# State space on Trainium2: imaginary coefficients and gate weights' low parts on GpSimd, rotation and scan in place in a PSUM bank, last norm's mean taken off early

## The chip, the cores and the metric

One Trainium2 chip, one core of it. The metric is the device time of one launch in microseconds. A core has five engines, each with an instruction list of its own that it works through in order: TensorE (PE, matmuls), VectorE (DVE), ScalarE (ACT), GpSimd (POOL) and SyncE (SP), which here issues every DMA. They wait for one another by semaphores. Matmuls write into eight PSUM banks of 128 x 512 fp32 (`bank0` to `bank7` in the rows); in this kernel GpSimd works on tiles in SBUF alone.

## What is computed

A sequence of 512 tokens with 1024 channels goes through two blocks of two layers each. The change touches the first layer's mixer, a state-space model, and the last layer norm.

```python
u = h @ w_in
a = exp(lam * step)
b, c = f(lam, step) * b, c
x[l] = a * x[l - 1] + b @ u[l]
y = real(c @ x) + d_skip * u
z = gelu(y)
val, gate = split(z @ w_glu)
x = x + val * sigmoid(gate)
...
h = layernorm(DEEPNORM_ALPHA * h + y, ln_g[layer], ln_b[layer])
```

Here `a`, `b`, `c` and the state are complex, with 64 groups of 16 channels and 64 states in each. The layer norm subtracts the mean over the 1024 channels, divides by the standard deviation, scales by `ln_g` and adds `ln_b`.

## The kernel before, in words

Activations lie with channels on partitions: eight tiles `x0` to `x7` of 128 x 512. A large matmul is done as three fp32r passes, hi x hi, lo x hi and hi x lo: the hi part of a weight (`wh`) is a ScalarE copy to fp32r, the lo part (`wl`) a VectorE subtraction (`wconv`, line 615), from the raw weights (`wr`, two buffers) that a DMA brings (`wload`).

**State space.** The projection by `w_in` has eight blocks of 128 channels. Blocks 0 to 2 are multiplied in plain fp32 from raw weights, with no wait for the first norm; blocks 3 to 7 take the three passes. Block m's result is scaled by the norm into `u` (VectorE), written to DRAM and read back in another layout. The scan over 512 tokens is cut into 64 chunks of 8. For each of the eight groups of channels m the kernel builds:
- P[m] and Q[m] (`s5_p`, `s5_q` through `s5_cprod`, line 965), powers of `a` times `b` and `c`. Each is four products of 128 x 512, two for the real part and two for the imaginary part, and two additions or subtractions. The products go into a ring of four buffers (tag `s5t`; in the order below `s5_45`, `s5_46`, `s5_53`, `s5_54`), and read the powers from bank 7, where ScalarE has copied them. `Bt` and `Ct` (`s5_58`, `s5_59` for even m, `s5_61`, `s5_62` for odd m) hold `b` and `c`.
- K[m], eight small matmuls of `Bh` (`s5_60`, `s5_63`) with Q[m], and P[m] transposed by eight PE transposes through a bank that ScalarE empties.
- `s5_x` (line 1049): the chunk inputs, 16 small matmuls into bank 6; a rotation by tables of cosine and sine that turns the complex recurrence into a real one; one scan over the chunks; a rotation back, giving the state `st`. Each rotation is two VectorE products and two GpSimd halves.
- `s5_y`: K[m] and `st` with Q[m] times `u`, in PE; then `s5_o`, the transposes back and the gelu. `glu_part` multiplies with `w_glu` as the groups become ready, its weights split in `load_glu` (line 1208).

The tables (`s5_table`, line 929), four in all, are built on GpSimd by doubling, one for two groups: at each step two products and two halves, up to 512 wide. The first norm's inverse root is GpSimd's power (`rsqrt`, line 737; tile `sm4_r1`, `sm_r` in the profile); PE spreads it over the partitions by four transposes, and VectorE needs it for `u`.

**What sets the order.** All instructions of the program are first collected by the class `Plan`, which estimates each one's duration and due time, and then lists them engine by engine: what stands in an engine's list is not the order in which the code is written. Everything is issued from one line, L263, so the profile's rows tell groups apart by tile and shape, not by line. A moved or retyped instruction can therefore move others in all five lists.

**The last norm.** `ln_half` (line 1721) runs for the two halves of the tokens. PE sums x and its squares over channels by matmuls with `ones`; VectorE forms mean and variance; GpSimd takes the power; VectorE multiplies by the mean; four transposes spread the inverse root and the product mean x inverse root. Then for each chunk x is multiplied by the first and the second is subtracted (on GpSimd for the first chunk, else on VectorE), ScalarE applies gain and bias, and a DMA stores it.

Of the kernel before, what the change touches and what calls it, by code (L numbers as in the profile page):

```python
# [20 lines left out]
P = 128  # L21
# [505 lines left out]
class Net:  # L527
# [86 lines left out]

    def wconv(self, raw, ncol, gain=None, cuts=1):
        nc = self.nc
# [8 lines left out]
        for c in range(0, ncol, w):  # L625
            p = slice(c, c + w)
            nc.scalar.activation(hi[:, p], raw[:, p], AF.Copy)
            nc.vector.tensor_tensor(lo[:, p], raw[:, p], hi[:, p], ALU.subtract)
        return hi, lo
# [334 lines left out]

    def s5_cprod(self, pool, out, x, tb, op0, op1, swap, E):


        V = self.nc.vector

        def prod(r, q):  # L970
            t = pool.tile([P, 4, 8, 16], F32, name=self.n("t"), tag="s5t", bufs=4)
            V.tensor_tensor(t, tb[:, :, q].unsqueeze(3).to_broadcast([P, 4, 8, 16]),
                            x[:, :, r].unsqueeze(2).to_broadcast([P, 4, 8, 16]), ALU.mult)
            return t.rearrange("p w j k -> p w (j k)")
# [4 lines left out]
        yield  # L979
        a, b = prod(1, 0), prod(0, 1)  # L980
        yield
# [4 lines left out]
    def s5_q(self, pool, m, ld):  # L986

        q = pool.tile([P, 4, 2, P], F32, name=self.n("Q"), tag="s5Q", bufs=3)
        return q, self.s5_cprod(pool, q, ld[1], self.powers[:, 1, m % 4 * 4 : m % 4 * 4 + 4], ALU.add, ALU.subtract, True,
                                (self.nc.vector, self.nc.gpsimd))  # L990

# [57 lines left out]
    def s5_x(self, pool, m, us, pt):  # L1049
# [68 lines left out]
    def layer0_mix(self, pool):  # L1118
# [602 lines left out]
    def ln_half(self, pool, h, g, b, hs=None, out=None):  # L1721

        nc, V, G = self.nc, self.nc.vector, self.nc.gpsimd
        p = self.psum("o")
        pairs = [(0, self.acc["s"]), (1, self.acc["n"])]
# [22 lines left out]
        for m in range(KC):  # L1748
# [524 lines left out]
```

## Time and profile before

| | us |
|---|---|
| median of 3 runs | 1833.55 (1832.9 to 1834.58) |
| the profiled execution's own time | 1832.58 |
| its span in the trace | 1830.8 |
| PE busy | 1788.1 (98%) |
| VectorE busy | 1153.1 (63%) |
| ScalarE busy | 840.9 (46%) |
| GpSimd busy | 431.3 (24%) |
| mean granted PE clock, of 2.4 GHz | 0.994 |

The span is what the trace shows; the profiled execution's own time holds 1.8 us more around it and lies 1.0 us below the median. Busy shares are means over the whole program: GpSimd's 24% is nearly 100% from 30 to 120 us and little after 160. The state-space stage takes about the first 156 us; from there PE is hardly ever idle until the last 10 us.

### The profile page before, as it was taken

How to read it: one execution, taken by the hardware profiler on the slowest of the kernel's cores; microseconds unless marked ns; L12 is line 12 of the kernel's file. 1: busy time of each engine (PE TensorE's matmuls, PEld its weight loads, DVE VectorE, ACT ScalarE, POOL GpSimd, SP SyncE). 2: the span in 40 equal slices, each digit the busy share in tenths (PEclk: the TensorE clock that was granted, in tenths of full speed). 3: DMA queues.
4: the chain of work that ended last, by engine and by line, in shares of the span. 5: the costliest groups of instructions: out<-in, count | busy, mean ns of one | idle time of the engine just before them, and what ended most of it. 6: DMA issues, size and time to landing. Idle time of an engine off the chain costs nothing.

```text
span 1830.8 us, 26476 instructions
## 1 busy us (share of the span) xinstructions
PE 1788.1 (98%) x10020; PEld 1448.8 (79%) x10020; DVE 1153.1 (63%) x2344; ACT 840.9 (46%) x1603; POOL 431.3 (24%) x518
## 2 busy tenths in 40 slices
PE   7999999999999999999999999999999999999997
PEld 4767888888888776678888888897878898878877
DVE  9994364344355688755444434583897875498886
ACT  4333332122223477734322223364677745476764
POOL 7981111001012176611100101230022030012104
PEclk8999999999999999999999999999999999999999
DMA  4542332332323220022233333332122122211113
GB/s 133 148 105 88 93 101 92 94 99 87 101 91 93 84 81 17 23 75 92 93 92 93 94 102 92 101 117 93 58 70 71 58 92 93 88 52 58 59 64 110
DMA packets 73135, 157.84 MB, mean 86 GB/s; under 512 B 26416, under 2 KB 34864, under 8 KB 73008
## 3 DMA queue, kind: packets, MB, share of 16 engines
q1 hardware_dynamic: 73008, 156.15, 27.7%
q8 instruction: 79, 1.29, 0.3%
q14 instruction: 48, 0.39, 0.1%
HBM read 150.81 MB, written 4.72 MB: 85 GB/s over the span
## 4 chain that ended last, share of the span: by engine, by line
PE 79%; DVE 9%; ACT 4%; POOL 2%; issue 1%; DMA 1%; SPq 0%; ACTq 0%; DVEq 0%; POOLq 0%
PE bank L263 79%; DVE bl L263 3%; DVE wl_r L263 1%; ACT bl L263 1%; DVE s L263 1%; ACT bh L263 1%; DVE x L263 1%; ACT wh_r L263 1%; DVE ml L263 1%; ACT ml L263 1%; DMA wr_r<-w_out 0%; POOL yq_r L263 0%; DVE bank L263 0%; POOL s L263 0%; POOL sm_r L263 0%
## 5 line engine op out<-in xcount | busy, mean ns | idle before, releaser
L263 ACT ACTIVATE wh_r<-wr_r 128x1024 fp32r<-128x1024 f32 (+2 forms) x269 | 277.4, 1031 | 586.8 <-PE bank L263 538.5
L263 PE MATMUL bank<-xl_r,wh_r 128*128 128x512 f32 (+1 forms) x1304 | 498.7, 386 | 0.0
L263 PE MATMUL bank<-xh_r,wl_r 128*128 128x512 f32 (+1 forms) x1304 | 497.7, 385 | 0.5 <-DVE wl_r L263 0.4
L263 PE MATMUL bank<-xh_r,wh_r 128*128 128x512 f32 (+1 forms) x1304 | 496.3, 386 | 0.8 <-ACT wh_r L263 0.7
L263 DVE TENSOR_TENSOR wl_r<-wr_r,wh_r 128x1024 fp32r<-128x1024 f32 (+2 forms) x269 | 367.0, 1365 | 152.5 <-ACT wh_r L263 144.9
L263 PEld LDWEIGHTS bank<-xh_r,wl_r 128*128 128x128 f32 x1304 | 245.4, 189 | 53.6 <-issue 3.8
L263 PEld LDWEIGHTS bank<-xh_r,wh_r 128*128 128x128 f32 x1304 | 245.1, 189 | 53.3 <-ACT wh_r L263 1.8
L263 PEld LDWEIGHTS bank<-xl_r,wh_r 128*128 128x128 f32 x1304 | 245.5, 189 | 50.4 <-issue 2.3
L263 PE MATMUL bank<-ff,wh_r 128*128 128x512 f32 (+1 forms) x816 | 226.1, 365 | 0.3 <-ACT ff L263 0.3
L263 DVE TENSOR_TENSOR ff<-bank,ff 128x512 f32<-128x512 f32 x88 | 60.9, 692 | 224.3 <-PE bank L263 224.2
L263 POOL TENSOR_TENSOR ff<-ff,ff 128x512 f32<-128x512 f32 x44 | 62.6, 1424 | 591.2 <-DVE ff L263 576.0
L263 PE MATMUL bank<-bh,wh_r 128*128 128x512 f32 (+1 forms) x656 | 171.8, 349 | 1.4 <-ACT wh_r L263 1.2
L263 PEld LDWEIGHTS bank<-ff,wh_r 128*128 128x128 f32 x816 | 145.6, 188 | 28.0 <-DVE ff L263 1.0
L263 POOL TENSOR_TENSOR acc_r<-acc_r,sq_r 128x256 f32<-128x256 f32 (+1 forms) x63 | 78.5, 1247 | 305.4 <-ACT sq_r L263 251.8
L263 PE MATMUL bank<-ff,wl_r 128*128 128x512 f32 (+1 forms) x408 | 146.8, 364 | 0.4 <-DVE wl_r L263 0.4
L263 DVE TENSOR_TENSOR x<-x,bank 128x256 f32<-128x256 f32 (+1 forms) x112 | 57.5, 531 | 128.3 <-PE bank L263 128.3
L263 PEld LDWEIGHTS bank<-bh,wh_r 128*128 128x128 f32 x656 | 111.5, 188 | 16.7 <-ACT wh_r L263 1.7
L263 POOL TENSOR_TENSOR s<-s,s 128x512 f32<-128x512 f32 (+6 forms) x136 | 108.4, 827 | 19.1 <-DVE s L263 16.7
L263 PE MATMUL bank<-bh,wl_r 128*128 128x512 f32 (+1 forms) x328 | 112.0, 351 | 0.0
L263 ACT ACTIVATE ff<-ff 128x512 f32<-128x512 f32 x88 | 55.1, 627 | 74.4 <-POOL ff L263 68.9
L263 PEld LDWEIGHTS bank<-ff,wl_r 128*128 128x128 f32 x408 | 76.2, 188 | 13.9 <-DVE wl_r L263 0.6
L263 POOL TENSOR_TENSOR bl<-bl,bh 128x512 f32<-128x512 f32 x16 | 20.7, 1292 | 254.2 <-DVE bl L263 244.4
(272 smaller groups left out, 2753.8 us busy)
## 6 DMA issues: line engine op xcount, KB each, us to landing
wr_r<-w_gu SPq DMA_DIRECT2D x88, 512.0 KB, 3.5
wr_r<-w_in2f SPq DMA_DIRECT2D x48, 512.0 KB, 3.3
wr_r<-w_dn SPq DMA_DIRECT2D x37, 448.0 KB, 3.3
wr_r<-w_out SPq DMA_DIRECT2D x22, 512.0 KB, 3.3
wr_r<-w_dn SPq DMA_DIRECT2D x16, 512.0 KB, 3.5
wr_r<-w_in2v SPq DMA_DIRECT2D x16, 512.0 KB, 3.7
wr_r<-w_glu SPq DMA_DIRECT2D x12, 512.0 KB, 3.5
wr_r<-w_o SPq DMA_DIRECT2D x8, 512.0 KB, 3.3
```

Source lines behind the costliest of these rows:

```text
L263: lambda: f(*[real(v) for v in a], **{x: real(v) for x, v in k.items()}), load, rows, idle))
```

## The change

1. `load_glu`: the eight `wl` of the `w_glu` parts (128 x 512) go from VectorE to GpSimd.
2. `s5_q`: both products of Q's imaginary part go to GpSimd, which reads the powers from SBUF (`af`, `s5_52` in the order) instead of bank 7; the addition of Q's real part goes to GpSimd, too. P stays as it was.
3. `s5_x`: ScalarE builds a tile `sg` with minus sine and sine (two copies of 128 x 256 per group). Each rotation is now three VectorE operations of 128 x 512, two of them in place in bank 6; the scan runs in place there; the four GpSimd halves per group go.
4. The second half of the last norm has a function of its own, `ln_last`. Two more matmuls spread the sum of x over all partitions; VectorE subtracts the mean while the power is under way; two transposes instead of four, one multiplication per chunk, and gain and bias on VectorE for three of the eight chunks.

```diff
-    def wconv(self, raw, ncol, gain=None, cuts=1):
+    def wconv(self, raw, ncol, gain=None, cuts=1, eng=None):
...
-            nc.vector.tensor_tensor(lo[:, p], raw[:, p], hi[:, p], ALU.subtract)
+            (eng or nc.vector).tensor_tensor(lo[:, p], raw[:, p], hi[:, p], ALU.subtract)
...
-    def s5_cprod(self, pool, out, x, tb, op0, op1, swap, E):
+    def s5_cprod(self, pool, out, x, tb, op0, op1, swap, E, sb=None):
...
-        def prod(r, q):
+        def prod(r, q, V=V, tb=tb):
...
-        a, b = prod(1, 0), prod(0, 1)
+        by = (V, tb) if sb is None else (self.nc.gpsimd, sb)
+        a, b = prod(1, 0, *by), prod(0, 1, *by)
...
-                                (self.nc.vector, self.nc.gpsimd))
+                                (self.nc.gpsimd, self.nc.gpsimd), self.af[:, 4 * m : 4 * m + 4])
...
+        sg = pool.tile([P, 4, 2, NCH], F32, name=self.n("sg"), tag="s5sg", bufs=2)
+        nc.scalar.activation(sg[:, :, 0], tab[:, :, 1], AF.Copy, scale=-1.0)
+        nc.scalar.activation(sg[:, :, 1], tab[:, :, 1], AF.Copy)
         yield
-        a, b, y, z = tmp("ra"), tmp("rb"), tmp("ry"), x4
+        a = tmp("ra")
         V.tensor_tensor(a, x4, cs, ALU.mult)
-        V.tensor_tensor(b, x4, sn, ALU.mult)
-        G.tensor_tensor(y[:, :, 0], a[:, :, 0], b[:, :, 1], ALU.add)
-        G.tensor_tensor(y[:, :, 1], a[:, :, 1], b[:, :, 0], ALU.subtract)
+        V.tensor_tensor(x4, x4, sg, ALU.mult)
+        V.tensor_tensor(x4, x4, a[:, :, ::-1], ALU.add)
         yield
         f = lambda v: v.rearrange("p j r c -> p (j r c)")
-        V.tensor_tensor_scan(xp, f(dz), f(y), 0.0, ALU.mult, ALU.add)
+        V.tensor_tensor_scan(xp, f(dz), xp, 0.0, ALU.mult, ALU.add)
         yield
-        a2, b2 = tmp("ra"), tmp("rb")
-        V.tensor_tensor(a2, z, cs, ALU.mult)
-        V.tensor_tensor(b2, z, sn, ALU.mult)
+        a2 = tmp("ra")
+        V.tensor_tensor(a2, x4, cs, ALU.mult)
+        V.tensor_tensor(x4, x4, sg, ALU.mult)
         l = slice(0, NCH - 1)
-        G.tensor_tensor(st[:, :, 0, 1:], a2[:, :, 0, l], b2[:, :, 1, l], ALU.subtract)
-        G.tensor_tensor(st[:, :, 1, 1:], a2[:, :, 1, l], b2[:, :, 0, l], ALU.add)
+        V.tensor_tensor(st[:, :, :, 1:], x4[:, :, :, l], a2[:, :, ::-1, l], ALU.add)
...
-            wa[k] = self.wconv(raw, S)
+            wa[k] = self.wconv(raw, S, eng=G)
...
+        if h and out is not None:
+            yield from self.ln_last(g, b, out)
+            return
...
+    def ln_last(self, g, b, out):
...
+        for a, src in enumerate((self.acc["s"], self.acc["x"])):
+            nc.tensor.matmul(sx[:, :256], self.ones.to_broadcast([P, P]), src[:, t], start=a == 0, stop=a == 1)
...
+        self.rsqrt(r, v)
+        rb = self.psum("s")
+        for i in range(2):
+            nc.tensor.transpose(rb[:, i * P : (i + 1) * P], r[:, i : i + 1].to_broadcast([P, P]), self.ident)
+        nc.urgent = False
+        for m in range(KC):
+            x = self.x[m][:, t]
+            V.scalar_tensor_tensor(x, sx[:, :256], -1.0 / D, x, ALU.mult, ALU.add)
+        for m in range(KC):
+            yield
+            x = self.x[m][:, t]
+            V.tensor_tensor(x, x, rb[:, :256], ALU.mult)
+            if m in (2, 5, 7):
+                V.tensor_scalar(x, x, self.col(g, m), self.col(b, m), ALU.mult, ALU.add)
+            else:
+                nc.scalar.activation(x, x, AF.Identity, bias=self.col(b, m), scale=self.col(g, m))
+            nc.sync.dma_start(out[m][:, t], x)
```

The plan turns this into other lists on every engine. Three places of them matter below. In the rows, `wr_r0_5` and `wr_r1_29` are the two buffers for raw weights, and what stands in brackets is what an instruction waits for: queues of DMAs, or the engines (`Activation` is ScalarE).

**SyncE, after the loads of the first inputs.** In the list before, the raw weights of blocks 2, 3, 4 and 5 of `w_in` stand one behind the other, and only then comes the next `Bt`:

```order
L263 DMA wr_r0_5_87<-w_in 128x1024 [waits DMAHW1_49,PE_49]
L263 DMA wr_r1_29_95<-w_in 128x1024 [waits DMAHW2_49,PE_49]
L263 DMA wr_r0_5_87<-w_in 128x1024 [waits DMAHW3_49,DMAHW1_49,PE_49]
L263 DMA wr_r1_29_95<-w_in 128x1024 [waits DMAHW4_49,DMAHW2_49,DVE_49]
L263 DMA s5_58_298<-Bt 128x128 [waits DMAHW5_49,DVE_49]
```

In the changed list these are the loads of block 2, then `Bt` and `Ct` for group 2, then blocks 3 and 5, `Bt` for group 3, and blocks 7 and 4:

```order
L263 DMA wr_r0_5_87<-w_in 128x1024 [waits DMAHW1_49,PE_49]
L263 DMA s5_58_298<-Bt 128x128 [waits DMAHW2_49,DVE_49]
L263 DMA s5_59_299<-Ct 128x128 [waits DMAHW3_49,DVE_49,Pool_49]
L263 DMA wr_r1_29_95<-w_in 128x1024 [waits DMAHW4_49,PE_49]
L263 DMA wr_r1_29_95<-w_in 128x1024 [waits DMAHW5_49,DMAHW4_49,DVE_49]
L263 DMA s5_61_301<-Bt 128x128 [waits DMAHW6_49,DVE_49]
L263 DMA wr_r1_29_95<-w_in 128x1024 [waits DMAHW7_49,DMAHW5_49,DVE_49]
L263 DMA wr_r0_5_87<-w_in 128x1024 [waits DMAHW1_49,DMAHW0_49,PE_49]
```

Block 3's load (waiting only for PE, which has read block 1 from that buffer) now stands behind a load that waits for VectorE and GpSimd, and block 4's behind that of block 7, which waits for VectorE.

**GpSimd, around the first norm's power** (`sm4_r1`). Before, the power stands between the two last 512-wide products of the first table (`s5_56`, `s5_57`; the table is `s5_24`), and the two additions for P[0] (into `s5_64`) follow it:

```order
L263 TENSOR_TENSOR s5_56_296<-s5_24_264,s5_42_282 128x512 [waits DVE_49,Pool_49]
L263 TENSOR_TENSOR sm4_r1_76_115<-sm4_r0_74_114,mhalf_81 128x4 [waits DVE_49]
L263 TENSOR_TENSOR s5_57_297<-s5_24_264,s5_42_282 128x512
L263 TENSOR_TENSOR s5_64_304<-s5_45_285,s5_46_286 128x4x128 [waits DVE_49]
L263 TENSOR_TENSOR s5_24_264<-s5_56_296,s5_57_297 128x8x32 [waits Pool_49]
L263 TENSOR_TENSOR s5_56_296<-s5_25_265,s5_42_282 128x32 [waits Pool_49]
L263 TENSOR_TENSOR s5_24_264<-s5_56_296,s5_57_297 128x8x32
L263 TENSOR_TENSOR s5_57_297<-s5_25_265,s5_42_282 128x32 [waits Pool_49]
L263 TENSOR_TENSOR s5_64_304<-s5_53_293,s5_54_294 128x4x128 [waits DVE_49]
L263 TENSOR_TENSOR s5_25_265<-s5_56_296,s5_57_297 128x8x2 [waits Pool_49]
```

After the change, the two rows of 512 and the real addition of P[0] are already past when this piece begins; the power follows the whole first table and the first products of the second (`s5_25`), and behind it come the two imaginary products of Q[0] (`s5_53` and `s5_54` from `s5_52` and `Ct`, `s5_59`):

```order
L263 TENSOR_TENSOR s5_24_264<-s5_56_296,s5_57_297 128x8x32 [waits Pool_49]
L263 TENSOR_TENSOR s5_56_296<-s5_25_265,s5_42_282 128x32 [waits Pool_49]
L263 TENSOR_TENSOR s5_24_264<-s5_56_296,s5_57_297 128x8x32
L263 TENSOR_TENSOR s5_57_297<-s5_25_265,s5_42_282 128x32 [waits Pool_49]
L263 TENSOR_TENSOR sm4_r1_76_115<-sm4_r0_74_114,mhalf_81 128x4 [waits DVE_49]
L263 TENSOR_TENSOR s5_25_265<-s5_56_296,s5_57_297 128x8x2 [waits Pool_49]
L263 TENSOR_TENSOR s5_64_304<-s5_53_293,s5_54_294 128x4x128
L263 TENSOR_TENSOR s5_25_265<-s5_56_296,s5_57_297 128x8x2
L263 TENSOR_TENSOR s5_53_293<-s5_52_292,s5_59_299 128x512 [waits DMAHW0_49,Pool_49]
L263 TENSOR_TENSOR s5_56_296<-s5_25_265,s5_42_282 128x64 [waits Pool_49]
L263 TENSOR_TENSOR s5_57_297<-s5_25_265,s5_42_282 128x64
L263 TENSOR_TENSOR s5_54_294<-s5_52_292,s5_59_299 128x512
```

The power has moved back by six operations, the products of Q[0] are new, and the real and the imaginary addition of Q[0] (`s5_28`) follow 13 and 18 operations behind the last row, the real and imaginary additions of P[1] 34 and 36 behind it.

**VectorE, behind the first norm.** Before, the four products of Q[0] with its real addition, the `wl` of blocks 4 and 5 and the first products of P[1]:

```order
L263 TENSOR_TENSOR s5_45_285<-bank7_76,s5_59_299 128x512 [waits DMAHW1_49,Activation_49,Pool_49]
L263 TENSOR_TENSOR s5_46_286<-bank7_76,s5_59_299 128x512
L263 TENSOR_TENSOR s5_32_272<-bank0_69,s5_35_275 128x512 [waits DVE_49]
L263 TENSOR_TENSOR wl_r1_137_123<-wr_r0_5_87,wh_r1_135_122 128x1024 [waits DMAHW4_49,DMAHW5_49,DMAHW3_49,Activation_49]
L263 TENSOR_TENSOR s5_53_293<-bank7_76,s5_59_299 128x512 [waits Pool_49]
L263 TENSOR_TENSOR s5_28_268<-s5_45_285,s5_46_286 128x4x128 [waits DVE_49]
L263 TENSOR_TENSOR s5_54_294<-bank7_76,s5_59_299 128x512
L263 TENSOR_TENSOR wl_r2_144_126<-wr_r1_29_95,wh_r2_142_125 128x1024 [waits DMAHW4_49,Activation_49]
L263 TENSOR_TENSOR s5_45_285<-bank7_76,s5_61_301 128x512 [waits Activation_49]
L263 TENSOR_TENSOR s5_46_286<-bank7_76,s5_61_301 128x512
```

Now, from the `wl` of block 3 (`wl_r0`) on:

```order
L263 TENSOR_TENSOR wl_r0_130_120<-wr_r1_29_95,wh_r0_128_119 128x1024 [waits DMAHW4_49,Activation_49]
L263 TENSOR_TENSOR s5_45_285<-bank7_76,s5_61_301 128x512 [waits DMAHW2_49,Pool_49]
L263 TENSOR_TENSOR s5_46_286<-bank7_76,s5_61_301 128x512 [waits DVE_49]
L263 TENSOR_TENSOR s5_53_293<-bank7_76,s5_61_301 128x512 [waits Pool_49]
L263 TENSOR_TENSOR s5_54_294<-bank7_76,s5_61_301 128x512
L263 TENSOR_TENSOR wl_r2_144_126<-wr_r1_29_95,wh_r2_142_125 128x1024 [waits DMAHW5_49,Activation_49]
L263 COPY s5_35_275<-bank6_75 128x512 [waits PE_49]
L263 TENSOR_TENSOR s5_32_272<-bank0_69,s5_35_275 128x512 [waits DVE_49]
L263 TENSOR_TENSOR s5_33_273<-bank1_70,s5_35_275 128x512
L263 TENSOR_TENSOR s5_45_285<-bank7_76,s5_62_302 128x512 [waits Activation_49,Pool_49]
L263 TENSOR_TENSOR s5_46_286<-bank7_76,s5_62_302 128x512
L263 TENSOR_TENSOR wl_r1_137_123<-wr_r0_5_87,wh_r1_135_122 128x1024 [waits DMAHW1_49,DMAHW3_49,DMAHW0_49,Activation_49]
```

The `wl` of block 5 (`wl_r2`) has come ahead of the one of block 4 (`wl_r1`), and stands behind products of P[1] into `s5_53` and `s5_54`, which wait for GpSimd to have read these two buffers for Q[0]; the `wl` of block 4 stands behind the real products of Q[1], which wait for GpSimd's real addition of P[1].

## Rows read from the trace of the kernel before

**Rows 1.** The page, part 1: busy us, share of span, instructions per engine.
```profile
PE 1788.1 (98%) x10020; PEld 1448.8 (79%) x10020; DVE 1153.1 (63%) x2344; ACT 840.9 (46%) x1603; POOL 431.3 (24%) x518
```
**Rows 2.** Windows: stretch, us, busy PE, PEld, DVE, ACT, POOL (x), PEclk, DMA share, GB/s.
```profile
30.00:38.60 8.60, 0.50 (x2) 0.19 (x1) 8.53 (x23) 0.67 (x1) 8.21 (x11) 0.74 0.17 62
38.60:45.00 6.40, 6.32 (x19) 5.05 (x20) 5.85 (x10) 3.48 (x6) 6.24 (x8) 0.55 0.29 94
60.00:100.00 40.00, 36.57 (x422) 26.92 (x422) 38.98 (x59) 12.29 (x26) 38.67 (x51) 1.00 0.46 117
100.00:156.00 56.00, 52.12 (x709) 40.65 (x705) 45.65 (x63) 18.54 (x33) 38.06 (x44) 0.97 0.36 95
156.00:1820.00 1664.00, 1650.30 (x8703) 1351.26 (x8699) 1007.17 (x2028) 780.24 (x1491) 306.37 (x349) 1.00 0.27 83
```
**Rows 3.** Waits of PE from 20 to 160: us in total, times, longest.
```profile
PE bank L263 <- POOL sm_r L263: 7.5, 1, 7.5
PE bank L263 <- DVE s L263: 3.9, 4, 1.4
PE bank L263 <- ACT s L263: 2.5, 1, 2.5
```
**Rows 4.** Timeline at the start: start us, us, engine; in brackets, idle before and releaser.
```profile
29.62 1.04 ACT L263 ACTIVATE wh_r<-wr_r 128x1024 fp32r<-128x1024 f32 x1
...
37.16 1.47 POOL L263 TENSOR_TENSOR sm_r<-sm_r,mhalf 128x4 f32<-128x4 f32 x1
...
38.68 1.11 PE L263 MATMUL bank<-ident,sm_r 128*128 128x128 f32 x4 [7.47 <-POOL sm_r L263]
```
**Rows 5.** Timeline: loads of `w_in` by SyncE (SPq), and the first `wl`.
```profile
21.39 0.33 SPq L263 DMA_DIRECT2D wr_r<-w_in  x1
...
38.61 1.21 DVE L263 TENSOR_TENSOR wl_r<-wr_r,wh_r 128x1024 fp32r<-128x1024 f32 x1
39.85 0.33 SPq L263 DMA_DIRECT2D wr_r<-w_in  x1
```
**Rows 6.** DMA issues up to 70 us: KB each, median us from issue to landing.
```profile
wr_r<-w_in SPq DMA_DIRECT2D x7, 512.0 KB, 3.6
```
**Rows 7.** Timeline of GpSimd: one row per shape, and three longer ones.
```profile
38.60 2.12 POOL L263 TENSOR_TENSOR s<-s,s 128x512 f32<-128x512 f32 x1
...
40.69 1.57 POOL L263 TENSOR_TENSOR s<-s,s 128x512 f32<-128x512 f32 x1
...
42.21 0.74 POOL L263 TENSOR_TENSOR s<-s,s 128x256 f32<-128x256 f32 x1
...
45.51 1.23 POOL L263 TENSOR_TENSOR s<-s,s 128x16 f32<-128x16 f32 x1
...
47.00 0.30 POOL L263 TENSOR_TENSOR s<-s,s 128x64 f32<-128x64 f32 x1
...
48.09 0.25 POOL L263 TENSOR_TENSOR s<-s,s 128x32 f32<-128x32 f32 x1
...
49.86 0.41 POOL L263 TENSOR_TENSOR s<-s,s 128x128 f32<-128x128 f32 x1
...
50.22 1.31 POOL L263 TENSOR_TENSOR s<-s,s 128x512 f32<-128x512 f32 x1
```
**Rows 8.** Groups by form, 40 to 156, GpSimd and VectorE: busy us, mean ns.
```profile
L263 POOL TENSOR_TENSOR s<-s,s 128x512 f32<-128x512 f32 x31 | 44.3, 1434 | 1.5 <-DVE s L263 0.8 <-PE bank L263 0.4
...
L263 DVE TENSOR_TENSOR s<-bank,s 128x512 f32<-128x512 f32 x102 | 64.4, 678 | 3.4 <-ACT bank L263 1.5 <-POOL s L263 1.4 <-PE bank L263 0.2
```
**Rows 9.** Timeline of PE: block 4's third matmul, and the stage's last small matmuls.
```profile
48.06 0.39 PE L263 MATMUL bank<-xh_r,wl_r 128*128 128x512 f32 x1
...
152.99 3.15 PE L263 MATMUL bank<-s,s 128*64 128x128 f32 x48
```
**Rows 10.** Timeline of the tail: the last power, and the last scalings on ScalarE.
```profile
1820.69 0.72 POOL L263 TENSOR_TENSOR sm_r<-sm_r,mhalf 128x2 f32<-128x2 f32 x1 [2.22 <-DVE sm_r L263]
...
1823.37 4.42 ACT L263 ACTIVATE x<-x,cols 128x256 f32<-128x256 f32 x8 [0.84 <-POOL x L263]
```

More of the change, by code (lines that the diff above doesn't have):

```diff
@@ L1059, in s5_x @@
         tab = self.tab[m // 2][:, 4 * (m % 2) : 4 * (m % 2) + 4]
-        cs, sn = (tab[:, :, a : a + 1].to_broadcast([P, 4, 2, NCH]) for a in range(2))
+        cs = tab[:, :, 0:1].to_broadcast([P, 4, 2, NCH])
         tmp = lambda nm: pool.tile([P, 4, 2, NCH], F32, name=self.n(nm), tag="s5" + nm, bufs=1)
@@ L1739, in ln_half @@
         V.tensor_tensor(c[:, 2:4], mu, c[:, 0:2], ALU.mult)
-        if h and out is not None:
-            nc.behind(self.stored)
         yield
@@ L1762, in ln_half @@
             V.tensor_tensor(lo, x, hi, ALU.subtract)
+    def ln_last(self, g, b, out):
+        nc, V = self.nc, self.nc.vector
+        t = HALF[1]
+        sx = self.psum("s")
+        p = self.psum("o")
+        for a, src in enumerate((self.acc["s"], self.acc["x"])):
+            nc.tensor.matmul(sx[:, :256], self.ones.to_broadcast([P, P]), src[:, t], start=a == 0, stop=a == 1)
+        pairs = [(0, self.acc["s"]), (1, self.acc["n"]), (0, self.acc["x"]), (1, self.acc["q"])]
+        for a, (j, src) in enumerate(pairs):
+            for i in range(2):
+                nc.tensor.matmul(p[:, 2 * j + i : 2 * j + i + 1], src[:, (2 + i) * P : (3 + i) * P],
+                                 self.ones, start=a == i == 0, stop=a == 3 and i == 1)
+        yield
+        nc.urgent = True
+        mu, m2, v, r = (self.small(2) for _ in range(4))
+        V.tensor_scalar(mu, p[:, 0:2], 1.0 / D, None, ALU.mult)
+        V.tensor_scalar(v, p[:, 2:4], 1.0 / D, LN_EPS, ALU.mult, ALU.add)
+        V.tensor_tensor(m2, mu, mu, ALU.mult)
+        V.tensor_tensor(v, v, m2, ALU.subtract)
+        nc.behind(self.stored)
+        self.rsqrt(r, v)
+        rb = self.psum("s")
+        for i in range(2):
+            nc.tensor.transpose(rb[:, i * P : (i + 1) * P], r[:, i : i + 1].to_broadcast([P, P]), self.ident)
[4 more added lines that the diff above has]
+        for m in range(KC):
+            yield
+            x = self.x[m][:, t]
[5 more added lines that the diff above has]
+            nc.sync.dma_start(out[m][:, t], x)
     def halves(self, add, order, pool, g, b, hs=None, out=None, nxt=None):
```

## The prediction

> **What bounds the kernel now.** The page first: TensorE (PE) is busy 98% of the span [rows 1], so a change counts only where PE waits, runs at its lower clock, or is handed work later. Next the waits by stage: after 156 us PE idles 13.7 of 1664 us [rows 2], so what the state-space stage gains or loses before 156 reaches the end one for one. In that stage PE idles 8.1 us from 30 to 38.6, runs to 45 at a mean granted clock of 0.55 (a mixture of 1.2 and 2.4 GHz, right behind the idle stretch), and then idles 3.4 us from 60 to 100 and 3.9 us from 100 to 156, with the clock at 0.97 in the last stretch [rows 2]. Its longest wait, 7.5 us, is for GpSimd's power that ends the first norm (`sm_r`); the later ones are mostly for VectorE (3.9) and once for ScalarE (2.5) [rows 3]. GpSimd is the other full engine: 38.7 of 40 us from 60 to 100, 38.1 of 56 after that [rows 2]. Last come single rows of the start, because the order of four queues changes there.
>
> **The start: a queue is blocked.** Before, the raw weights of block 3 of `w_in`, the first that is split, are asked for at 21.39 [rows 5]; their high part is on ScalarE at 29.62 and PE only lacks the norm, whose power runs 37.16 to 38.6 [rows 4]. That SyncE issues strictly in turn is seen at 39.85: the next load starts as `wl` ends (38.61 + 1.21) [rows 5]. After the change the load of block 3 stands behind that of `Ct`, which waits until GpSimd has read the old `Ct` in both imaginary products of Q[0]. Those are new on GpSimd. So I walk GpSimd's list.
>
> The power starts later by what is now ahead of it: the second 512-wide table product (2.12), the real add of P[0] (1.57), two halves of 256 (0.74 each) and two products of 32 (0.25 each) [rows 7], 5.7 us. One sum of squares goes ahead of the tables into idle time; I credit one 512-wide row, 1.3. Start 37.16 + 5.7 - 1.3 = 41.5. It took 1.47 here and 0.72 in the tail [rows 4, 10]; with 1.1 it ends at 42.6. From there to the second product of Q[0] the list has three operations of 512 (1.31 each), two of 64 (0.30) and two of 16 (at most the 0.25 of a 32) [rows 7]: 5.0, so 47.6. Two issues of 0.33 follow one another; the load lands 3.6 after its own issue [rows 5, 6], at 51.6; `wh` takes 1.04 [rows 4]. Block 3 starts at **52.7**; before, all but its first matmul followed the stall that ended at 38.68 [rows 4].
>
> The second hold is block 4. Its load now stands behind the load of block 7, which waits for VectorE's `wl` of block 5, and that stands behind P[1]'s imaginary products, which wait for buffers until GpSimd's imaginary add of Q[0]. From 47.6 to that add GpSimd has four operations of 512, four of 256, four of 128, two of 64 and four of 32, at 1.31, 0.74, 0.41, 0.30 and 0.25 [rows 7]: 11.4, so 59.0. To the real add of P[1] come two of 512, two of 256, four of 128, four of 64 and four of 32 or less: 7.9, so 66.9. On VectorE: 59.0, two products of 0.68 [rows 8], `wl` of 1.21 [rows 5], 61.6; load issued and landed 65.5; `wh` 66.6. The `wl` of block 4 stands behind Q[1]'s real products, which wait for the real add of P[1]: 66.9 + 2 x 0.68 + 1.21 = **69.5**.
>
> At 69.5 PE starts block 4's third matmul. Before it did so at 48.06 [rows 9]. PE is then ahead by K[0] and half of P[1]'s transposes: eight small matmuls at 3.15/48 us each [rows 9] and four transposes of at most 1.11 [rows 4], some 1.0 us together with what is halved. Delay: 69.5 - 49.1 = 20.4. What PE lost later before can be recovered: 7.3 of idle time and 0.03 of 52 us of clock, 1.6 [rows 2]. That leaves 11.5. New waits are next: K[1] needs seven more 512-wide GpSimd operations (66.9 + 9.2 = 76.1), about 1 us beyond PE's own work. VectorE gets to the first rotation only after P[2]'s imaginary products, which wait for that same add; counting from there its twelve rows at 0.68, one `wl` at 1.21 and the scan at twice 0.68, the first state is ready near 87, while 45 matmuls of 512 columns (0.21 each at 2.4 GHz), some 67 small ones at 3.15/48 and the 1 us bring PE there about 84.5: 1.5 to 2.5, of which I take the lower, as consecutive rows overlap. Sum for the stage: **+14**. The last small matmuls of the stage, at 152.99 before [rows 9], would run near 167.
>
> **The steady part.** Per group of channels GpSimd loses four rotation halves (at most 4 x 0.74) and gains two products, one add and one `wl`, four rows of 512 (5.2): +2.3, or some 18 us over eight groups. From 60 to 156 it has 19.3 us idle [rows 2], so it fits, with nothing left over; VectorE is the cover for PE here, no longer GpSimd. VectorE loses two products, an add and a `wl` and gains two adds: -1.4 by its 0.68. No row has a VectorE operation that reads and writes a bank; below, one costs like the read alone (0.68), above I double it, since both ends are banks. I take 0.68, the nearest row; doubled, four per group add 2.7 us to VectorE, which rival 3 takes up. The new ScalarE copies (two of 256 columns) are hidden beside the two thirds of the stage in which ScalarE idles [rows 2], except the four at the start, which stand ahead of the first `wh`; the blocked load covers them.
>
> **How fast is GpSimd beside VectorE?** The clean 512-wide row is 1.31, the mean in the stage 1.43 [rows 7, 8]; a 16-wide one took 1.23 [rows 7] where VectorE subtracted two SBUF tiles. I use clean rows, since the change leaves VectorE few operations with two SBUF inputs; by the mean 21 of them to K[1] cost 2.5 more, which goes into the upper end. The Trainium skill (SBUF — State Buffer, section Who interferes with whom) says that a VectorE instruction with two SBUF inputs and a GpSimd one that reads SBUF exclude each other, and that one with at most one SBUF input does not contend. The 1.23 agrees; by that rule the sum stands at clean rows, +14, and by the mean at +16.5.
>
> **The tail.** The mean is subtracted while the power (0.72) runs, so behind it come one multiply per chunk and the output scaling, of which three of eight leave ScalarE; its eight took 4.42 [rows 10]. Three fewer would be 1.7 less. Two more matmuls of 256 columns and eight subtractions stand ahead or beside. I take -1.0, between -2 (the scaling's part and the removed copy) and +0.5 (nothing saved, the matmuls added).
>
> **Sum.** +14 - 1 = +13. The profiled execution took 1832.6, 1.8 outside its span of 1830.8, and lies 1.0 below the median of 1833.55; it would become 1845.6, the median **1846**.
>
> **Rivals.** (1) Only the first hold counts, if blocks 4 and later are never late: PE starts block 3 at 52.7, 13.2 behind where it resumed, recovers 8.9 and gains 1 in the tail: +3.5, 1837. For it: 20 GpSimd rows could be shorter; against: three queues agree on the second hold.
> (2) **Faster.** VectorE's relief decides: two products, an add and a `wl` less per group remove the 7.3 idle and 1.6 of clock, while the start costs nothing because GpSimd passes Q[0]'s products in time. The turning point: the products would have to end near 43, not 47.6, for the hold to be below the 8.9 recovered, and the second hold would have to vanish. Then 1833.6 - 8.9 - 1 = 1824. The Trainium skill's rule on the two engines (SBUF — State Buffer, Who interferes with whom) is on this side: fewer exclusions for both. Against it: before 42 VectorE's work is the same small SBUF operations, so GpSimd is not relieved there.
> (3) GpSimd becomes the bound to the end: 18 us more work in 19.3 of slack, started 5 us late. If its last add comes after 150 and the bank operations cost double, PE waits some 8 us more: 1854.
>
> **How the numbers follow.** A measurement of this kernel can tell about 0.2%, 3.7 us, from no change. Chances: forecast 0.80, rival 1 0.09, rival 2 0.05, rival 3 0.06. Within the forecast the lower end has the short power and the two long rows at 1.31 (1.4 less together), no new waits and the whole tail (11.5 - 1.4 - 2: 1842), the upper the mean GpSimd row (2.5), the restart at the low clock (0.45 of 6.4 us, 2.9) and no tail gain (14 + 5.4: 1853). From 1838 to 1853 leaves out rival 2, half of rival 1 and most of rival 3. Slower: 0.90 (forecast, rival 3, half of 1); same 0.05; faster 0.05.
>
> **What would show it.** Right: the wait of the first matmul with `wh` names ScalarE's `wh` or the load, and ends near 52; the load of block 3 is issued near 48 just as a GpSimd product ends; block 4 near 67; two long idle stretches of PE between 30 and 70; few idle gaps of PE from 90 to 165. Wrong: a load of `w_in` issued before 40 among the `Ct` loads, or the last small matmuls before 160.

## The result, and the profile after

The changed kernel takes **1848.61 us** (median of 4, 1847.72 to 1850.48), the kernel before, on the same chip, 1834.07: a ratio of 1.0084, 95% interval 1.0072 to 1.0096. Slower, by about the forecast amount (1846, range 1838 to 1853). The profiled execution took 1849.37 us, its span is 1847.6, 16.8 more than before. The sum came out; that the late start is its only cause did not, as the experiments show.

The page's first part, of the kernel after, beside [rows 1]:

```profile
PE 1791.2 (97%) x10022; PEld 1451.9 (79%) x10022; DVE 1138.6 (62%) x2331; ACT 844.1 (46%) x1615; POOL 432.0 (23%) x517
```

The sums hide everything: GpSimd's busy time is within 1 us of before (0.7 more), since it gained long products and lost short halves. The same stretches as [rows 2], after (columns: stretch, us, busy PE, PEld, DVE, ACT, POOL, PEclk, DMA share, GB/s):

```profile
30.00:38.60 8.60, 2.27 (x6) 0.72 (x4) 8.53 (x16) 0.00 (x0) 8.21 (x12) 0.86 0.00 1
38.60:45.00 6.40, 0.55 (x3) 0.56 (x4) 5.44 (x10) 2.54 (x7) 4.27 (x7) 0.50 0.04 10
60.00:100.00 40.00, 35.88 (x318) 26.65 (x318) 32.90 (x45) 13.93 (x29) 37.61 (x46) 0.91 0.59 158
100.00:156.00 56.00, 55.01 (x707) 42.70 (x707) 42.50 (x68) 21.64 (x45) 42.15 (x44) 1.00 0.44 112
156.00:1820.00 1664.00, 1650.07 (x8786) 1349.73 (x8783) 1000.44 (x2017) 776.89 (x1483) 295.61 (x340) 1.00 0.27 82
```

PE now stands nearly idle from 38.6 to 45, and has almost no gap from 100 to 156 (1.0 us; 3.9 before). The steady 1664 us are as before. PE's waits from 20 to 160, after, beside [rows 3]:

```profile
PE bank L263 <- POOL sm_r L263: 12.2, 1, 12.2
PE bank L263 <- ACT s L263: 7.1, 3, 5.9
PE bank L263 <- ACT wh_r L263: 6.9, 1, 6.9
```

The queue of the start, after: SyncE's loads, the power on GpSimd, the high and the low part of block 3's weights, and PE (start us, us; in brackets the idle time before and what ended it). The last row is the stage's last run of small matmuls of this shape:

```profile
43.25 0.33 SPq L263 DMA_DIRECT2D s<-Bt  x1
48.56 0.33 SPq L263 DMA_DIRECT2D s<-Ct  x1
48.98 6.28 SPq L263 DMA_DIRECT2D wr_r<-w_in  x2
61.63 0.33 SPq L263 DMA_DIRECT2D s<-Bt  x1
62.76 0.81 SPq L263 DMA_DIRECT2D wr_r<-w_in  x2
...
43.38 1.02 POOL L263 TENSOR_TENSOR sm_r<-sm_r,mhalf 128x4 f32<-128x4 f32 x1 [1.98 <-DVE sm_r L263]
52.57 1.06 ACT L263 ACTIVATE wh_r<-wr_r 128x1024 fp32r<-128x1024 f32 x1 [7.00 <-DMA wr_r<-w_in]
53.66 1.24 DVE L263 TENSOR_TENSOR wl_r<-wr_r,wh_r 128x1024 fp32r<-128x1024 f32 x1 [8.72 <-ACT wh_r L263]
...
44.45 1.12 PE L263 MATMUL bank<-ident,sm_r 128*128 128x128 f32 x4 [12.18 <-POOL sm_r L263]
53.68 0.80 PE L263 MATMUL bank<-xh_r,wh_r 128*128 128x512 f32 x1 [6.91 <-ACT wh_r L263]
62.49 1.11 PE L263 MATMUL bank<-ident,s 128*128 128x128 f32 x4 [5.89 <-ACT s L263]
72.34 0.50 PE L263 MATMUL bank<-xh_r,wl_r 128*128 128x512 f32 x1 [0.29 <-DVE wl_r L263]
...
168.77 2.99 PE L263 MATMUL bank<-s,s 128*64 128x128 f32 x48
```

These answer [rows 4, 5 and 9]: the load of block 3 at 48.98 right behind `Ct` (21.39 before), block 3 at 53.68, the next pair of loads at 62.76, block 4's third matmul at 72.34 (48.06), the last small matmuls of this shape at 168.77 (152.99).

**A marker for the stage's end.** The order of matmuls differs from kernel to kernel, so the n-th of the three-pass matmuls (those that read `wh` or `wl`) is comparable only where no small matmul is left. The 250th is behind all of them in every kernel here. It ends at 173.1 before and at 188.7 after: **+15.6**. At the last such matmul the distance is 16.5, and the tail adds 0.3: 16.8.

### The profile page after: what moved, and what is told of

Read it like the earlier page. It is cut to its first block, busy times and chain, and to the rows that moved or that the text cites. A ratio compares the mean times of both kernels' runs of the same rounds, so it can differ in the third digit from the quotient of the medians.

```text
span 1847.6 us, 26476 instructions
## 1 busy us (share of the span) xinstructions
PE 1791.2 (97%) x10022; PEld 1451.9 (79%) x10022; DVE 1138.6 (62%) x2331; ACT 844.1 (46%) x1615; POOL 432.0 (23%) x517
## 4 chain that ended last, share of the span: by engine, by line
PE 82%; DVE 8%; ACT 4%; POOL 3%; issue 1%; DMA 1%; SPq 0%; DVEq 0%; POOLq 0%; ACTq 0%
PE bank L263 81%; DVE bl L263 4%; POOL s L263 2%; DVE wl_r L263 1%; ACT bl L263 1%; DVE s L263 1%; DVE x L263 1%; ACT bh L263 1%; ACT wh_r L263 1%; ACT ml L263 0%; POOL sm_r L263 0%; POOL yq_r L263 0%; ACT xh_r L263 0%; DVE bh L263 0%; DVE ml L263 0%
## 5 line engine op out<-in xcount | busy, mean ns | idle before, releaser
L263 DVE TENSOR_TENSOR wl_r<-wr_r,wh_r 128x1024 fp32r<-128x1024 f32 (+1 forms) x261 | 360.0, 1380 | 158.2 <-ACT wh_r L263 150.6
L263 POOL TENSOR_TENSOR s<-s,s 128x512 f32<-128x512 f32 (+5 forms) x128 | 101.8, 820 | 8.2 <-DVE s L263 3.1
```

The costliest lines, as they stand in the source:

```text
L263: lambda: f(*[real(v) for v in a], **{x: real(v) for x, v in k.items()}), load, rows, idle))
```

## The experiments

Theory A is the forecast's: GpSimd's products of Q[0] hold `Ct`, `Ct` holds the loads of `w_in`, and this late start is the price. Theory B: GpSimd's list is too long for the stage, wherever the loads stand. All runs in one table; "ends" is the marker, "coefficients" the end of GpSimd's last operation on P, Q or a table.

| kernel | median us | ratio to before, 95% | ends | coefficients |
|---|---|---|---|---|
| before | 1834 to 1836 | 1 | 173.1 | 133.0 |
| the change | 1848.61 | 1.0084, 1.0072 to 1.0096 | 188.7 | 146.9 |
| `loads_first` | 1848.75 | 1.0076, 1.0059 to 1.0093 | 188.9 | 147.2 |
| `loads_all` | 1846.85 | 1.0062, 1.0047 to 1.0077 | 181.6 | 143.5 |
| `glu_back` | 1852.24 | 1.0093, 1.0078 to 1.0108 | 176.1 | 142.2 |
| `q_back` | 1829.82 | 0.9977, 0.9968 to 0.9986 | 169.6 | 130.4 |
| `after_nf` | 1849.42 | 1.0079, 1.0064 to 1.0094 | 189.6 | 147.8 |
| `loads_all_nf` | 1848.58 | 1.0069, 1.0052 to 1.0086 | 180.9 | 144.2 |
| `glu_back_nf` | 1857.11 | 1.0118, 1.0101 to 1.0135 | 176.2 | 142.5 |
| `q_back_nf` | 1829.26 | 0.9966, 0.9955 to 0.9978 | 172.1 | 131.5 |
| `q_late` | 1829.53 | 0.9977, 0.9967 to 0.9986 | 168.9 | 133.3 |
| `q_early` | 1831.42 | 0.9984, 0.9974 to 0.9994 | 170.1 | 133.2 |
| `rot_only` | 1831.58 | 0.9984, 0.9974 to 0.9993 | 173.0 | 133.3 |
| `q_early_held` | 1838.90 | 1.0021, 1.0011 to 1.0031 | 181.7 | 146.8 |

### The loads put back in order

`loads_first`: the change, with `Ct`, `Bt` and `Bh` of group 2 behind the loads of `w_in`'s blocks 3 and 4.

```diff
+        for i in self.loads[3:5] if m == 2 else ():
+            self.nc.behind(i)
         self.nc.sync.dma_start(bt, self.A["Bt"][:, g4])
```

> The whole change, with one thing added: the loads of Bt, Ct and Bh for group 2 are tied behind the loads of w_in's blocks 3 and 4. In SyncE's list block 3 then stands in front of Ct, but block 4 still stands behind block 7 and the Bt of group 3. Theory A (two holds in SyncE's list, of which the second sets the time): block 3 starts right behind the norm, at 44 to 46 instead of 53.7, block 4 still not before 66, and the time stays at 1844 to 1849. Rival B (GpSimd's longer list alone sets the time, whatever the loads do): 1846 to 1850. Rival C (the first hold is the whole cost): 1836 to 1840.

Measured: no change to the changed kernel. Block 3 starts at 46.9 instead of 53.7, and PE then waits longer for the next thing (its timeline in `loads_first`):

```profile
62.73 1.12 PE L263 MATMUL bank<-ident,s 128*128 128x128 f32 x4 [12.66 <-ACT s L263]
...
72.58 0.50 PE L263 MATMUL bank<-xh_r,wl_r 128*128 128x512 f32 x1 [0.29 <-DVE wl_r L263]
```

The first hold alone costs nothing: block 4 is as late as in the change (72.58 to 72.34). Rival C falls; theories A and B both allow this time.

`loads_all`: the loads of blocks 3 to 7 in turn, those of the groups 2 and 3 behind block 4.

```diff
+        if 5 <= len(getattr(self, "loads", [])) < 8:
+            self.nc.behind(self.loads[-1])
...
+        for i in self.loads[3:5] if m in (2, 3) else ():
+            self.nc.behind(i)
```

> The whole change, with the loads of w_in's blocks 3 to 7 tied to one another in turn and those of groups 2 and 3 behind block 4: in SyncE's list blocks 2, 3, 4 and 5 stand one behind the other as in the kernel before. Theory A (the order of the loads costs the time, the work on GpSimd does not): block 4's third matmul comes before 58 instead of 72.3, the long idle stretches of PE after the norm go, and the time is 1825 to 1834, at or below the kernel before. Rival B (GpSimd's longer list sets it): K[0] and P[1] still wait for GpSimd, 1843 to 1849.

Measured: theory A falls, as far as it makes the late start the whole price. Block 4's third matmul is at 51.5, 3.4 us behind before, and yet the stage ends 8.5 late and the kernel is 0.62% slower than before. The delay of 24 us at this matmul is gone but for 3.4, and most of the price by the median, half of it at the marker, is still there.

`glu_back` and `q_back`: one part of the change undone each.

```diff
-            wa[k] = self.wconv(raw, S, eng=G)
+            wa[k] = self.wconv(raw, S)
```

> The change without its first part: the low parts of the gate weights' eight tiles stay on VectorE. The coefficients of Q stay on GpSimd, the rotation stays in place. In this kernel's list the loads of blocks 3, 5 and 4 stand in front of the Ct that waits for GpSimd, though nothing before 100 us is different in the work. Theory A (the order costs the time): 1826 to 1836. Rival B (Q's coefficients on GpSimd cost it): 1843 to 1849. Rival D (the eight low parts on GpSimd cost it): 1830 to 1836 as well, but then with the idle gaps after 100 us that go and not those before 72.

```diff
-                                (self.nc.gpsimd, self.nc.gpsimd), self.af[:, 4 * m : 4 * m + 4])
+                                (self.nc.vector, self.nc.gpsimd))
```

> The change without its second part: Q's four products and its real addition stay on VectorE. The loads of blocks 3, 5 and 4 stand in front of the next Bt and Ct in SyncE's list. Theory A: 1826 to 1836, as with the loads put in order. Rival B (GpSimd's coefficients): 1826 to 1834 as well. Rival E (the rotation and scan in place cost time): 1840 to 1848, with VectorE rows that write a bank well above 0.7 us.

Without Q's part the kernel is faster than either, 0.9977 of before: the whole loss hangs on Q. Rival E falls; A and B expected nearly the same time here, so the run does not decide between them. `glu_back` is slower than all three of its expected ranges. It gives 12.6 us back at the marker (176.1) and loses them later: its last three-pass matmul comes 18.8 behind before's. At the marker it is 3.0 behind before, with all of Q on GpSimd and no held load.

### Are the spare products to blame?

Where the plan expects PE to wait it lists spare products, identity by identity, into a bank about to be written. Before has 50 of them, the change 50, `loads_all` 108, `glu_back` 170. (The sums of durations in the expectations count overlaps twice; by the busy rows before's 50 take 7.3 us.) In `glu_back`, PE's groups of that line:

```profile
L276 PE MATMUL bank<-ident 128*128 128x128 f32 x110 | 15.0, 276 | 0.0
L276 PE MATMUL bank<-ident 128*128 128x1 f32 x34 | 4.5, 234 | 0.0
L276 PE MATMUL bank<-ident 128*64 128x128 f32 x26 | 4.1, 284 | 0.0
```

So the same four kernels were run with these left out (they compute nothing that is used):

```diff
-            for _ in range(n):
-                self.ops[j][8][1]()
```

> The change, without the spare products. The plan puts spare products of the identity (ident x ident, into a bank that is about to be written) into TensorE's list where it expects a wait: 50 in the kernel before and 50 in the change (13.8 us busy in each), but 108 (28.5 us) in loads_all and 170 (45.7 us) in glu_back, by the traces of those runs. Here they are left out of the list and everything else stays in its order. Theory F (they lie where TensorE would work, so they cost time and hide what the two runs gave back): 1838 to 1846, since 50 of them stand in both kernels alike. Theory W (they lie on waits that are there anyway): 1846 to 1852, and higher if the granted clock falls where they stood.

> loads_all (every load of w_in's blocks in turn, groups 2 and 3 behind block 4) without the spare products. 42 of its 108 stand between 100 and 200 us, 10.3 us busy, where the change has none. Theory F with theory A (the late loads are the cost of the change, and the spare products hid what the order gave back): 1830 to 1838, the three-pass matmul 250 at 172 to 176. Theory B (GpSimd's work on Q ends late and TensorE waits for it wherever the loads stand): 1844 to 1849, the matmul 250 at 180 to 183, and TensorE waiting some 8 us more between 100 and 170 us.

> The change with the low parts of the gate weights back on VectorE, without the spare products (170 of them, 45.7 us, in glu_back, most of them between 650 and 1850 us). Theory F: 1828 to 1840, and the loss of 15 us that glu_back had after the 4000th three-pass matmul is gone. Theory W: 1848 to 1855.

> The change with Q's imaginary part back on VectorE and GpSimd as before, without the spare products (56, 15.2 us, in q_back). Theory F: 1816 to 1825. Theory W: 1827 to 1834.

Measured: theory F falls in all four. Three lie within 1.8 us of their twins and within the ranges of theories W and B; `glu_back_nf` is 4.9 us slower than its twin, 2 us above W's range. The spare products hid nothing. Without them the traces show bare waits. Windows of `loads_all_nf`:

```profile
60.00:100.00 40.00, 39.09 (x417) 29.16 (x415) 32.98 (x50) 13.97 (x31) 37.84 (x45) 1.00 0.54 136
100.00:156.00 56.00, 48.94 (x616) 35.92 (x617) 37.01 (x53) 17.60 (x37) 39.74 (x51) 0.94 0.27 72
```

PE runs through until 100, having had its blocks early, and then idles 7.1 of 56 us with the clock at 0.94: the work that was moved up is missing later, and the groups that could fill the place come late. And `after_nf`, then `glu_back_nf`, from 200 to 1820:

```profile
200.00:1820.00 1620.00, 1601.39 (x8388) 1309.63 (x8387) 979.15 (x1990) 760.12 (x1459) 290.81 (x338) 1.00 0.26 82
```

```profile
200.00:1820.00 1620.00, 1584.85 (x8261) 1295.84 (x8260) 980.78 (x1975) 756.91 (x1451) 289.05 (x333) 0.99 0.26 81
```

In a part that no edit touched, `glu_back_nf` idles 16.5 us more. The plan orders the whole program at once, so an edit at the start gives other lists hundreds of microseconds later. Why these are worse stays open; it means that `glu_back` can be read at the marker, not at the end.

### Half of Q, early or late

`q_late` leaves Q's new split to the groups 4 to 7, `q_early` (`m < 4`) to the groups 0 to 3. `rot_only` is the kernel before with the rotation of the change's diff alone.

```diff
-                                (self.nc.gpsimd, self.nc.gpsimd), self.af[:, 4 * m : 4 * m + 4])
+                                (self.nc.gpsimd if m >= 4 else self.nc.vector, self.nc.gpsimd),
+                                self.af[:, 4 * m : 4 * m + 4] if m >= 4 else None)
```

> The change with Q's new split for the groups 4 to 7 alone; the groups 0 to 3 as before. In the list no load of w_in stands behind Ct of the next group. Theory A (the late start of the stage is the cost): like q_back, 1826 to 1832. Theory B (GpSimd's list is full through the stage, and what is added to it comes out at the end): half of the added 27 us, but in q_back GpSimd is busy 23 of the 60 us from 100 to 160 us, so the added work has room there while VectorE, full until 130 us, is relieved: 1822 to 1830. Theory R (each added us of GpSimd costs, wherever it stands): about half of the 19 us between q_back and the change, 1836 to 1842.

> The mirror of q_late: Q's new split for the groups 0 to 3 alone. The raw weights of blocks 3 and 4 stand ahead of Ct of the next group in SyncE's list, so nothing holds them. Theory A: no hold, like q_back, 1826 to 1832. Theory B: 13.5 us are added where GpSimd has some 8 us of room (35.4 us busy of 40 from 60 to 100 in q_back, 5 us less than full in the 40 us ahead of that), so 5 to 10 us come out late: 1833 to 1841, with the fourth group's scan at 110 or later (106.7 in q_back, 123.8 in the change). Theory R: 1836 to 1842.

> The kernel before with the rotation and the scan in place in the bank, and nothing else of the change. GpSimd loses 32 halves of 0.74 us (24 us); VectorE gains two operations of 0.69 us a group less what its scan loses (1.43 to 1.22 us), 9 us in all; ScalarE gains 16 copies. Theory B (GpSimd bounds the stage before, too): the last scan some 5 us earlier than 150.2, 1824 to 1831. Theory V (VectorE is as full as GpSimd from 60 to 120 us, 59 of 60 us, and takes the work): no change to 5 us slower, 1834 to 1840.

Measured: half of Q costs nothing on either side; both are slightly faster than before. Theory R (each microsecond of GpSimd costs) falls. B's price for `q_early` falls too, A's for both fits: but `loads_all` has no held load either (its `Ct` for group 2 is issued at 51.0, that of `q_early` at 51.4) and is slow. What separates them, besides the ties on the loads, is how much of Q GpSimd has. Windows of `q_early`, beside those of `loads_all_nf` above:

```profile
60.00:100.00 40.00, 38.80 (x430) 29.32 (x427) 37.03 (x57) 14.95 (x33) 36.82 (x45) 1.00 0.59 146
100.00:156.00 56.00, 52.47 (x728) 40.07 (x726) 45.72 (x68) 21.20 (x42) 29.91 (x40) 1.00 0.28 79
```

GpSimd has 29.9 us to do after 100 instead of 39.7, and its coefficients end at 133.2 instead of 144.2. With half of Q the last coefficient comes within 0.3 us of before (133.0), and the stage ends no later. A late last coefficient does not by itself fix the stage's end, though: in `glu_back` it is 9.2 late and the marker 3.0.

`rot_only` takes GpSimd's halves away and leaves the marker where it was (173.0); by the median, 1831.58, between its two expected ranges, it gains 2.6 us. Its windows say why GpSimd's relief does not show:

```profile
60.00:100.00 40.00, 35.94 (x406) 27.57 (x404) 38.20 (x59) 13.12 (x30) 32.77 (x52) 0.96 0.50 127
100.00:130.00 30.00, 26.54 (x400) 20.32 (x399) 30.00 (x52) 11.23 (x25) 14.37 (x12) 1.00 0.26 73
```

VectorE is now full (30.0 of 30 us) and GpSimd half idle (14.4): with Q where it was, VectorE is the full engine.

### The hold by itself

`q_early_held` puts the hold into `q_early`: the loads of `w_in` from block 3 on stand behind `Ct` of group 2.

```diff
         self.nc.sync.dma_start(ct, self.A["Ct"][:, g4])
+        if m == 2:
+            self.held = self.nc.last()
+            for i in self.loads[3:8]:
+                self.nc.ops[i][3].setdefault(self.held, 0.0)
```

> q_early with the hold put in: w_in's raw weights from block 3 on stand behind Ct of group 2, as in the change, while GpSimd's list is 12 us shorter than the change's. Block 4's third matmul then comes at 68 to 73, as in the change (72.3; 47.8 before). Theory H (the forecast's: the late start by itself delays the stage by some 14 us, wherever GpSimd stands): 1842 to 1847, three-pass matmul 250 at 183 to 187 (170.1 in q_early, 188.7 in the change). Theory B2 (the stage ends when GpSimd's list does; with half of Q there is room, and most of the late start is caught up, since P, Q and K do not wait for the blocks): 1831 to 1837, matmul 250 at 171 to 177. In between (hold 7 us, as between the change and loads_all): 1838 to 1840, matmul 250 at 177 to 180.

Its loads on SyncE:

```profile
48.56 0.53 SPq L263 DMA_DIRECT2D s<-Ct  x1
...
49.73 1.15 SPq L263 DMA_DIRECT2D wr_r<-w_in  x2
```

`Ct` is issued to the hundredth where the change issues it, the loads 0.8 later, and the first three-pass matmul runs at 55.8 (53.7 in the change). Block 4's third matmul comes at 64.4, not at 68 to 73 as expected, so this hold is milder than the change's. The median is 7.5 us above that of `q_early`; by the ratios, 1.0021 to 0.9984, it is 6.8. Neither the forecast's price (H) nor none (B2), but the middle case that the expectation named. The marker, at 181.7, moved 11.6, more than the medians and than the middle case, but the profiled execution of `q_early`, at 1827.61, lies at the low end of its runs (1827.54 to 1832.72), and that of `q_early_held`, at 1840.94, is the highest of its own. The coefficients end at 146.8, as late as in the change, though only half of Q is on GpSimd: their late end can come from the hold as well as from a long list.

## Why the prediction was right in its sum, and what it missed

**The walk through the queues held,** within 3 us. The power was forecast to run from 41.5 to 42.6 and ran from 43.38 to 44.40: GpSimd's list reached it at 41.4, and the rest is a wait for VectorE (its row: 1.98 us idle for `sm_r`). The second product of Q[0] ended at 48.5 (47.6), block 3 started at 53.68 (52.7); the imaginary sum of Q[0] ended at 60.3 (59.0), the real sum of P[1] at 69.0 (66.9), block 4's third matmul ran at 72.34 (69.5). From that delay, 24.3, PE had recovered 8.7 by the marker; the forecast took a delay of 20.4, recovered 8.9 and added 2.5 of new waits. So +15.6 instead of +14: a start 3.9 us later, and 2.3 us more recovered. That these errors nearly cancel is luck.

How late the groups are shows in the scans, one for each group. First and last start, in this order: before, the change, `loads_all`, `glu_back`, `q_early`, `q_early_held` (times in ns, shortest, median, longest; then starts in us):

```profile
L263 DVE TENSOR_TENSOR_SCAN bank<-s,s x8: 1223/1314/2300, 66.1 to 150.2; 128x512 f32<-128x512 f32 x8
L263 DVE TENSOR_TENSOR_SCAN bank<-s,bank x8: 1210/1219/1229, 85.5 to 165.6; 128x512 f32<-128x512 f32 x8
L263 DVE TENSOR_TENSOR_SCAN bank<-s,bank x8: 1219/1228/1229, 67.1 to 160.7; 128x512 f32<-128x512 f32 x8
L263 DVE TENSOR_TENSOR_SCAN bank<-s,bank x8: 1216/1224/1229, 74.3 to 154.1; 128x512 f32<-128x512 f32 x8
L263 DVE TENSOR_TENSOR_SCAN bank<-s,bank x8: 1212/1216/1229, 64.6 to 146.5; 128x512 f32<-128x512 f32 x8
L263 DVE TENSOR_TENSOR_SCAN bank<-s,bank x8: 1214/1220/1229, 57.7 to 158.1; 128x512 f32<-128x512 f32 x8
```

In the change the first scan is 19.4 us late and the last 15.4: the whole delay is there at the first group (the forecast had its state ready near 87), and none is added after it. So in the changed kernel itself the delay arises where the forecast put it. In `loads_all` the first is 1.0 late and the last 10.5: take the late start away, and a delay of 9.5 us builds up between the first group and the last instead. The two overlap.

**The step that failed** is "From 60 to 156 it has 19.3 us idle [rows 2], so it fits, with nothing left over". The late start hid it. The idle time is real, but most of it comes too late. GpSimd before, up to its last coefficient and from there on:

```profile
60.00:133.00 73.00, 67.04 (x810) 50.56 (x808) 71.70 (x103) 23.22 (x46) 69.14 (x84) 0.98 0.46 117
133.00:156.00 23.00, 21.64 (x318) 17.01 (x316) 12.93 (x19) 7.61 (x13) 7.60 (x10) 1.00 0.22 65
```

Ahead of 133 it had 3.9 us of room, not 19.3; the other 15.4 lie behind it, where coefficients would be late. What had to fit was mis-sized, too: from 60 to 156 GpSimd's busy time rises by 3.0 us (76.7 to 79.8), not by 18, since a product of Q took 1.05 us where the forecast had 1.31, and the rows that stayed became shorter. `loads_all` shows the consequence with the loads in order. GpSimd from 30 to its last coefficient, before and in `loads_all`:

```profile
30.00:133.00 103.00, 88.86 (x937) 67.16 (x936) 100.18 (x154) 32.74 (x63) 98.19 (x120) 0.93 0.47 123
30.00:143.50 113.50, 97.30 (x1002) 72.38 (x1002) 92.71 (x137) 36.74 (x78) 103.91 (x127) 0.91 0.41 107
```

The coefficients end 10.5 us late; 5.7 of these are work (98.2 to 103.9) and 4.8 idle time (4.8 to 9.6). So GpSimd is not fuller than before, 92% against 95%, and "GpSimd becomes the bound to the end" (rival 3) is not what the row shows. Of its idle time 8.4 us are waits for VectorE, and VectorE's own longest wait there is for ScalarE (100 to 165, `loads_all`; then the same wait in `q_early`):

```profile
DVE s L263 <- ACT s L263: 11.7, 4, 5.3
```

```profile
DVE s L263 <- ACT s L263: 2.8, 3, 2.3
```

Which list sets that slower pace, GpSimd's added work or the order of the engines' lists beside one another, stays open.

**What the parts cost,** by ratios, on 1834 us: all of Q instead of half, loads not held (`q_early` to `loads_all`), 0.78%, 14.3 us. The hold with half of Q, 6.8. Both, `q_early` to the change, 1.00%, 18.3: less than the sum. At the marker the first two are alike, 11.5 and 11.6, and both together 18.6; the rest of the 14.3 arises behind it, where the lists are ordered anew. So it is not shown which of the two is larger. Without a tie on the loads, and with the gate weights' low parts on VectorE, all of Q costs less: `glu_back` is 6 behind `q_early` at the marker. Taking the hold out of the change itself gave 4.0 us, and 1.8 without spare products, neither clear of the intervals (7.1 and 8.7 at the marker). What is shown is that the late start, the forecast's whole price, and all of Q on GpSimd, which it put at nothing, each cost time alone, and that together they cost less than their sum. Both delay the last groups of the stage, so a chain with one cause came out at the right sum.

**Costs of operations.** VectorE's in-place operations cost 0.69, so the lower bound was right and rival 3's doubling wrong. GpSimd's 512-wide rows came out below the clean row on the mean. Its groups from 40 to 156 after, beside [rows 8], and VectorE's:

```profile
L263 POOL TENSOR_TENSOR s<-s,s 128x512 f32<-128x512 f32 x53 | 66.0, 1263 | 5.9 <-DVE s L263 3.0 <-PE bank L263 2.0
...
L263 POOL TENSOR_TENSOR wl_r<-wr_r,wh_r 128x512 fp32r<-128x512 f32 x7 | 9.0, 1285 | 5.5 <-ACT wh_r L263 5.5
```

```profile
L263 DVE TENSOR_TENSOR s<-bank,s 128x512 f32<-128x512 f32 x67 | 43.8, 680 | 21.8 <-POOL s L263 16.3 <-PE bank L263 4.2 <-ACT bank L263 1.2
L263 DVE TENSOR_TENSOR bank<-bank,s 128x512 f32<-128x512 f32 x20 | 13.8, 690 | 0.1
L263 DVE TENSOR_TENSOR_SCAN bank<-s,bank 128x512 f32<-128x512 f32 x7 | 8.5, 1221 | 0.1
```

The mean of 1.43 fell to 1.26, so clean rows were the better choice. But the group now holds a new kind of row, 16 products of Q at a mean of 1.12. Its sums, by themselves, fell from 1.42 (24 of them) to 1.35 (31), with rows of up to 2.27 still among them. The first VectorE row shows the other side: its products wait 16.3 us for GpSimd (1.4 in [rows 8]).

**The tail** was taken at -1.0 and measured +0.3. Its rows, after, beside [rows 10]:

```profile
1838.37 0.71 POOL L263 TENSOR_TENSOR sm_r<-sm_r,mhalf 128x2 f32<-128x2 f32 x1 [3.80 <-DVE sm_r L263]
...
1840.32 2.58 ACT L263 ACTIVATE x<-x,cols 128x256 f32<-128x256 f32 x5 [4.66 <-DVE x L263]
1840.94 3.81 SPq L263 DMA_DIRECT2D out<-x  x8
...
1842.84 0.73 DVE L263 TENSOR_SCALAR x<-x,cols 128x256 f32<-128x256 f32 x2
```

From the start of the last three-pass matmul to the end of the last computed chunk it takes 9.2 us instead of 9.9: the saving was there, 0.8 of the forecast 1.0. But SyncE issues the eight stores one by one, 0.48 us each (3.81 / 8), until 1844.75, 1.2 us after the last chunk is ready (0.4 before). What was late next was the queue of stores, which the forecast had not counted.

## What to carry to other kernels

Idle time of an engine counts as room only ahead of the last thing that others wait for; look at its row up to that instruction, not at the stage. An experiment that removes a stall and leaves most of the loss has found a second delay that the first one covered, so test the stall with the other load lightened, too. Where one plan orders the whole program, compare kernels at a marker right behind the part that was edited, since what follows is ordered anew and can move by more than the edit is worth. Half of the new split of Q, in either half of the groups, with the rest of the change keeps its gains: `q_late` takes 0.9977 of before.

## What had not been expected of the hardware

A GpSimd product of 512 columns whose two inputs are both broadcast (the powers over the tokens, `Ct` over the powers) took 1.05 us where nothing held it up (up to 2.04 otherwise), a sum of the same size 1.26 to 1.32 and a `wl` 1.285, in every kernel that has them. The Trainium skill (GPSIMD Engine Reference, section 3.1 Elementwise — side-by-side cycle accounting) gives two-input operations about 2.6 cycles for an element at 1.2 GHz, by our estimate 1.1 us for 512 before the fixed part. The sums agree with that; the products lie under it, so the measurement decides. Whether reading by broadcast or multiplying instead of adding makes them cheaper is not shown. The scan that reads and writes one bank took 1.21 to 1.23 us, where the one that reads SBUF alone had taken 1.22 to 2.30.
